# A decoder layer on Trainium2: the mixers' output loop turned, gate steps placed later, the value bank copied whole, and score tiles finished beside the value projection

## The chip, the core and the metric

The kernel runs on one core of one Trainium2 chip. A core has engines that run side by side, each with its own queue of instructions: TensorE (PE in the profile) multiplies matrices and writes to PSUM, VectorE (DVE) and ScalarE (ACT) work elementwise on PSUM and SBUF, GpSimd (POOL) works elementwise, and SyncE (SP) issues the DMAs between DRAM and SBUF. They wait for each other by semaphores. The metric is device time in microseconds (us), the median of some runs. Lower is better.

## The reference, cut to what matters

One hybrid decoder layer over 1024 tokens of width 1024, batch 1, all in float32. An mLSTM of 4 heads of 128 and a forgetting attention of 8 heads of 64 stand side by side; their outputs, joined to 1024 columns, go through `w_out`. Then follow a cross attention into 256 memory tokens (4 heads of 256) and a squared-ReLU MLP.

```python
h = rmsnorm(x, ln1[l])
z = h @ w_in[l]
ml_qk, ml_v, ml_o, ml_i, ml_f, fx_q, fx_k, fx_v, fx_f = jnp.split(z, splits, axis=-1)
...
ig = ml_i + ml_b_i[l]
lf = jax.nn.log_sigmoid(ml_f + ml_b_f[l])
mh = mlstm_chunkwise(mq, mk, mv, ig, lf)          # gates by cumulative sums of lf
mh = mh * lax.rsqrt(jnp.mean(mh * mh, axis=-1, keepdims=True) + EPS) * ml_norm
ml_out = mh * jax.nn.sigmoid(ml_o)

flf = jax.nn.log_sigmoid(fx_f + fx_b_f[l])        # forgetting attention:
s = jnp.einsum('bqhd,bkhd->bhqk', qi, k) * scale  # scores
s = s + (ci[..., :, None] - cT[..., None, :])     # plus differences of the cumulative flf
s = jnp.where(qpos[:, None] >= kpos[None, :], s, -jnp.inf)
fx_out = einsum('bhqk,bkhd->bqhd', softmax(s), v)

x = x + jnp.concatenate([ml_out, fx_out], axis=-1) @ w_out[l]
x = x + cross_attention(rmsnorm(x, ln_x[l]), rmsnorm(mem, ln_mem[l]), w_xq[l], w_xkv[l], w_xo[l])
u = jax.nn.relu(rmsnorm(x, ln2[l]) @ w_ff1[l])
x = x + (u * u) @ w_ff2[l]
```

## The kernel before, in words

**Numbers and tiles.** Activations are held transposed, features on the 128 partitions and tokens along the free axis, in 8 tiles of 128 features and two halves (`hf`) of 512 tokens. Each float32 operand is split into a high part (ACT, lines 138 and 141) and a low part, the remainder (DVE, lines 139 and 142). A product is then three matmuls, low times high, high times low and high times high (`mm3`, lines 192 to 194). PSUM has eight banks of 128x512 under five names: sc (3), tp (2), mm, m2 and ov (1 each). `mm()` hands out banks by a list of names that the stages set. SBUF buffers rotate under tags: act (7 large ones), w4 (5), z4 (2), and r_a to r_y, of which r_a and r_y have one buffer and the others two. A tile that takes a buffer waits until the former tile in it is read for the last time, a DMA out of it included.

**Who orders the work.** The program is traced in the order of the code, and the framework's scheduler then orders each engine's instructions by what is ready and by priority. Inside `in_order()` compute instructions keep the order of the code on each engine. All loads and stores are issued on one queue, SP, in its own order: a DMA that waits for a buffer holds up those behind it.

**Stages.** First the normalised input, then `token_major` for the mLSTM's values, with `row_first` and `gate_rows` called between its blocks. The gate's log-sigmoid is a polynomial on DVE (lines 449 to 453); `gate_rows` transposes the gates on TensorE (lines 469 and 474) and scans them along the tokens; `gate_cols` (lines 494 and 495) turns them back and stores the split cumulative sums in DRAM (`decay`, line 500). `mem_prepare` normalises the memory tokens, in steps that are called between others. Then the four mLSTM heads: `ml_project` makes a head's projections and `ml_head` its scores and output. Its last part, per half, loads a factor row that went through DRAM (`facd`, line 635), scales (lines 638 and 639), splits and stores the result to `mix` (lines 642 and 643).

**Forgetting attention.** `slot()` (line 1001, under `in_order`) does one step of several pipelines: a tile's scores go to a score bank by `Tile.score` (lines 748 and 749), the next slot takes their row maximum (`top`, lines 755 and 758, the second being the minimum of two negated maxima of a tile in two parts), the one after exponentiates (`exp`, lines 761 and 763), then `scale` divides (lines 768, 769 and 772). `Values` transposes the probabilities (line 787), splits them (lines 138 and 139) and multiplies them with the values (line 807), four to eight key blocks adding up in the one bank ov, rows 0 to 63 from the values' high parts and rows 64 to 127 from their low parts. `fx_close` (lines 811 to 817) joins these: ACT copies the lower 64 rows to r_c (line 816), DVE adds them to the upper 64 rows in PSUM (line 817). `fx_store` (lines 819 to 823) stores the finished pair of heads to `mix`. A first run of 13 slots does scores only, beside the end of the mLSTM; then `token_major(a["w_fv"], ...)` (line 1067) projects the values of all 8 heads in two columns of eight blocks, which `fv_sink` splits and stores to DRAM (`fvd`, line 662). The normalised memory is loaded (`hmd`, line 1069, 2 MB), and then slots with values run on, each with a piece of filler: the memory's keys and values and the part of `w_out` that needs only the first five feature tiles (`out_unit`; its sums go to `x1d`, line 945). The filler's weights are split in halves by ACT and, in turn, GpSimd and DVE (lines 974 and 975). `fv_load` (line 846) reads a head's values back.

**The mixers' output and the cross attention.** The other three feature tiles of the mixed output are loaded (`mix_load`, line 867) and multiplied in `out_proj` (line 876): per half, 8 blocks of 9 matmuls, with a weight load of 128x768 (line 180) and a split for every second block. `full_sink` (lines 1095 to 1112) loads the block's row of `x1d` into one of three tags (line 1099), adds (line 1103), stores it (line 1104), splits it for the queries (lines 141 and 142) and adds its squares (line 241). `cross_head` (line 1119) projects the queries of one head and half, 24 matmuls for each of two feature tiles, loads the head's keys and values (lines 1132 and 1133), and makes scores, softmax and output. The MLP and the last norm follow; they make up the time from about 760 us on.

## Time and profile before

| | |
|---|---|
| Runs | 1524.34, 1520.54, 1520.23 us; median 1520.54 |
| The profiled execution's own time | 1521.71 us |
| Its span, first to last instruction | 1519.7 us |
| Mean granted TensorE clock | 0.997 of full speed |
| ScalarE, VectorE, GpSimd busy | 48%, 73%, 28% |
| DMA | 298.28 MB, 196 GB/s on average |

The profile is of one execution, traced by the hardware. A timeline row gives start and duration in us, the engine, the line of the kernel, the operation, output and inputs by the program's names, shape and count, and in square brackets the engine's idle time just before with the work that ended it. A row of waits says which operation of which line waited for what: us in total, how often, and the longest. A row by stretches gives for each engine its busy time with the number of instructions, then the granted clock, the DMA share and GB/s. Shown busy times of matmuls overlap, so a busy engine isn't one at its peak.

### The profile page before, as it was taken

How to read it: one execution, taken by the hardware profiler on the slowest of the kernel's cores; microseconds unless marked ns; L12 is line 12 of the kernel's file. 1: busy time of each engine (PE TensorE's matmuls, PEld its weight loads, DVE VectorE, ACT ScalarE, POOL GpSimd, SP SyncE). 2: the span in 40 equal slices, each digit the busy share in tenths (PEclk: the TensorE clock that was granted, in tenths of full speed). 3: DMA queues.
4: the chain of work that ended last, by engine and by line, in shares of the span. 5: the costliest groups of instructions: out<-in, count | busy, mean ns of one | idle time of the engine just before them, and what ended most of it. 6: DMA issues, size and time to landing. Idle time of an engine off the chain costs nothing.

```text
span 1519.7 us, 21937 instructions
## 1 busy us (share of the span) xinstructions
PE 1502.2 (99%) x7708; PEld 1259.2 (83%) x7708; DVE 1102.4 (73%) x1745; ACT 723.1 (48%) x1349; POOL 433.1 (28%) x497
## 2 busy tenths in 40 slices
PE   9999999999999999999999999999999999999997
PEld 8888888889898888788888888788888888888887
DVE  7676676665798875854457888888887788777765
ACT  7333343334678763644343456565566432222124
POOL 0003030413455441001100033343343544343312
PEclk9999999999999999999999999999999999999998
DMA  6332333436887958953334436776775965555623
GB/s 211 118 108 91 118 101 123 133 127 174 267 248 221 302 178 283 315 197 119 118 138 156 164 122 231 280 276 241 264 262 210 366 261 222 222 222 217 253 84 111
DMA packets 118673, 298.28 MB, mean 196 GB/s; under 512 B 13202, under 2 KB 27852, under 8 KB 112420
## 3 DMA queue, kind: packets, MB, share of 16 engines
q1 hardware_dynamic: 118276, 296.79, 56.5%
q8 instruction: 60, 0.98, 0.3%
q14 instruction: 49, 0.40, 0.1%
q10 hardware_dynamic: 288, 0.11, 0.0%
HBM read 200.13 MB, written 96.72 MB: 195 GB/s over the span
## 4 chain that ended last, share of the span: by engine, by line
PE 88%; DMA 6%; DVE 3%; ACT 2%; issue 1%; SPq 0%; POOLq 0%; POOL 0%; DVEq 0%; ACTq 0%
PE tp L192 8%; PE tp L194 8%; PE tp L193 8%; PE sc L192 6%; PE sc L194 6%; PE sc L193 6%; PE m L193 6%; PE m L194 6%; PE m L192 6%; PE mm L193 5%; PE mm L192 5%; PE mm L194 5%; PE ov L192 2%; PE ov L193 2%; PE ov L194 2%; PE ov L807 2%
## 5 line engine op out<-in xcount | busy, mean ns | idle before, releaser
L192 PE MATMUL tp<-act,wl 128*128 128x512 f32 (+1 forms) x456 | 178.6, 392 | 0.0
L193 PE MATMUL tp<-act,wh 128*128 128x512 f32 (+1 forms) x456 | 178.6, 392 | 0.0
L194 PE MATMUL tp<-act,wh 128*128 128x512 f32 (+1 forms) x456 | 178.5, 392 | 0.0
L138 ACT ACTIVATE wh<-wr 128x1024 fp32r<-128x1024 f32 (+3 forms) x100 | 96.1, 962 | 118.3 <-PE tp L194 36.9
L139 DVE TENSOR_TENSOR wl<-wr,wh 128x1024 fp32r<-128x1024 f32 (+3 forms) x100 | 116.4, 1165 | 18.7 <-ACT wh L138 18.1
L192 PE MATMUL mm<-act,wl 128*128 128x512 f32 (+1 forms) x328 | 126.0, 384 | 0.7 <-DVE r_d L1103 0.7
L193 PE MATMUL mm<-act,wh 128*128 128x512 f32 (+1 forms) x328 | 125.8, 384 | 0.0
L194 PE MATMUL mm<-act,wh 128*128 128x512 f32 (+1 forms) x328 | 125.5, 383 | 0.0
L193 PE MATMUL m<-act,wh 128*128 128x512 f32 (+1 forms) x312 | 119.1, 382 | 0.7 <-DMA act<-mix 0.7
L192 PE MATMUL m<-act,wl 128*128 128x512 f32 (+1 forms) x312 | 119.3, 382 | 0.4 <-DVE r_d L1103 0.4
L194 PE MATMUL m<-act,wh 128*128 128x512 f32 (+1 forms) x312 | 119.1, 382 | 0.0
L194 PEld LDWEIGHTS tp<-act,wh 128*128 128x128 f32 x456 | 85.7, 188 | 19.5
L192 PEld LDWEIGHTS tp<-act,wl 128*128 128x128 f32 x456 | 85.7, 188 | 19.1
L193 PEld LDWEIGHTS tp<-act,wh 128*128 128x128 f32 x456 | 85.8, 188 | 19.0
L192 PE MATMUL sc<-act,wl 128*128 128x512 f32 (+1 forms) x260 | 100.7, 387 | 0.0
L193 PE MATMUL sc<-act,wh 128*128 128x512 f32 (+1 forms) x260 | 100.5, 387 | 0.0
L194 PE MATMUL sc<-act,wh 128*128 128x512 f32 (+1 forms) x260 | 100.5, 387 | 0.0
L1451 POOL TENSOR_TENSOR z<-wr 128x256 f32<-128x256 f32 x56 | 53.6, 978 | 148.4 <-DMA wr<-w_ff2q 131.7
L138 ACT ACTIVATE w<-wr 128x768 fp32r<-128x768 f32 (+2 forms) x31 | 25.5, 824 | 132.1 <-PE tp L194 69.1
L138 ACT ACTIVATE wh<-z 128x1024 fp32r<-128x1024 f32 (+2 forms) x55 | 52.5, 956 | 64.5 <-POOL z L1451 28.9
L139 DVE TENSOR_TENSOR wl<-z,wh 128x1024 fp32r<-128x1024 f32 (+2 forms) x55 | 66.1, 1202 | 10.1 <-ACT wh L138 10.1
L192 PEld LDWEIGHTS mm<-act,wl 128*128 128x128 f32 x328 | 61.6, 188 | 13.1 <-DVE r_d L1103 1.2
(677 smaller groups left out, 4187.2 us busy)
## 6 DMA issues: line engine op xcount, KB each, us to landing
act<-right SPq DMA_DIRECT2D x35, 1024.0 KB
right<-r_d SPq DMA_DIRECT2D x70, 256.0 KB
right<-w SPq DMA_DIRECT2D x56, 256.0 KB
wr<-w_ff2q SPq DMA_DIRECT2D x28, 512.0 KB
act<-fqk SPq DMA_DIRECT2D x48, 256.0 KB
wr<-w_in SPq DMA_DIRECT2D x20, 512.0 KB
wr<-w_ff SPq DMA_DIRECT2D x20, 512.0 KB
fqk<-r_p SPq DMA_DIRECT2D x32, 256.0 KB
```

The source lines that it names most:

```text
L138: s.activation(hi, src, AF.Copy)
L139: return v.tensor_tensor(out=lo, in0=src, in1=hi.bitcast(F32), op=ALU.subtract)
L192: nc.tensor.matmul(ps, w[1], x[0], start=first, stop=False, skip_group_check=more)
L193: nc.tensor.matmul(ps, w[0], x[1], start=False, stop=False, skip_group_check=more)
L194: nc.tensor.matmul(ps, w[0], x[0], start=False, stop=last, skip_group_check=more)
L807: nc.tensor.matmul(self.ov[:, c0:], self.fv[:, self.j], t[:, c0:], start=self.j == 0 and t is self.p[1], stop=self.last and t is self.p[0])
L1451: g.tensor_tensor(out=o, in0=x, in1=y, op=op)
```

## The change

Four places are changed; the matmuls that are computed stay the same.

**Gates.** `gate_rows` is called one block later (5 in place of 4), and `gate_cols` becomes the first step of the generator that prepares the memory.

**Last mLSTM head and the value projection.** In the last head both factor rows are loaded at once into two buffers (r_a, r_d), and the second half's high part goes to r_e in place of r_y. `catch_up` tops, exponentiates and scales the score tiles in flight: once ahead of the value projection and twice in each of its columns, under `in_order`. The first head's values are loaded inside the second column, and the score inputs of later heads (`fx_step`) are issued after that load.

**Slots.** `fx_close` copies the whole bank on ACT (128 rows in place of 64) and returns the addition, which `slot` issues later, after the probabilities' split; it adds two SBUF tiles. The minimum of line 758 is a `tensor_scalar` in place of a `tensor_tensor`.

**Output and first queries.** The loop over blocks is outermost and that over halves innermost, so four weight loads serve both halves. Both halves' mixed tiles are loaded first. The first query weight is loaded before the last block, the first query projection uses a score bank, the first head's scores run in another order, and the norms' rows are made later, between the cross heads.

```diff
@@ -626,18 +626,20 @@
         rsqrt_cols(fac, sqs, 1.0 / P, 8)
         v.tensor_tensor(out=fac, in0=fac, in1=rd, op=ALU.mult)
         yield
+        end = hd == MLH - 1
+        fbs = [w2("a"), w2("d")] if end else [None, None]
+        at = facd[hd : hd + 1]
         for hf in range(2):
-            fb = w2("a")
-            at = facd[hd : hd + 1]
+            fb = fbs[hf] or w2("a")
             if hf == 0:
                 to_row(fb, fac, 8, at, sc)
-            else:
-                load(fb, at[:, TH:].broadcast_to([P, TH]))
+            if hf != end:
+                load(fbs[1] or fb, at[:, TH:].broadcast_to([P, TH]))
             yield
             y = nums[hf]
             v.scalar_tensor_tensor(out=y, in0=y, scalar=vec[:, VEC["ml_norm"] + hd : VEC["ml_norm"] + hd + 1], in1=fb, op0=ALU.mult, op1=ALU.mult)
             v.scalar_tensor_tensor(out=y, in0=og[:, hf * TH : hf * TH + TH], scalar=1.0, in1=y, op0=ALU.add, op1=ALU.mult)
-            yh, yl = w2("y", dt=F32R), y.bitcast(F32R)
+            yh, yl = w2("e" if end and hf else "y", dt=F32R), y.bitcast(F32R)
             split(yh, yl, y, 0.5)
             load(mix[hf, 0, :, hd], yh.bitcast(F32))
             load(mix[hf, 1, :, hd], yl.bitcast(F32))
@@ -684,10 +686,14 @@
 
     banks[:] = ["tp", "m2", "tp", "sc", "mm", "sc", "sc"]
     turn[0] = 0
-    token_major(a["w_mv"], mv_sink, (1,), {2: row_first, 4: gate_rows}, other)
-    gate_cols()
+    token_major(a["w_mv"], mv_sink, (1,), {2: row_first, 5: gate_rows}, other)
     banks[:] = ["mm", "tp", "m2", "tp"]
-    closing = mem_prepare()
+
+    def gates_then_memory():
+        gate_cols()
+        yield from mem_prepare()
+
+    closing = gates_then_memory()
     ready = ml_project(0)
     for hd in range(MLH):
         closing = ml_head(hd, *ready)
@@ -703,7 +709,7 @@
         g.memset(t[0:2, 3].bitcast(F32), 1.0)
         stacks.append(t)
 
-    coming = []
+    coming, fetched = [], []
 
     def fx_load(hd):
 
@@ -719,7 +725,8 @@
     def fx_step():
         if coming:
             dst, src = coming.pop(0)
-            load(dst.bitcast(F32), src)
+            with tc.issue_after(fetched[0]) if fetched else nullcontext():
+                load(dst.bitcast(F32), src)
 
     masks = []
 
@@ -755,7 +762,7 @@
             v.tensor_reduce(out=self.mxs[:, e : e + 1], in_=self.ps[e], axis=mybir.AxisListType.X, op=ALU.max, negate=True)
             if e:
 
-                v.tensor_tensor(out=self.mxs[:, 1:2], in0=self.mxs[:, 0:1], in1=self.mxs[:, 1:2], op=ALU.min)
+                v.tensor_scalar(out=self.mxs[:, 1:2], in0=self.mxs[:, 1:2], scalar1=self.mxs[:, 0:1], scalar2=None, op0=ALU.min)
 
         def exp(self, e):
             s.activation(self.pt[:, slice(*self.parts[e])], self.ps[e], AF.Exp, bias=self.mxs[:, e : e + 1], accum_out=self.dens[:, e : e + 1])
@@ -813,8 +820,8 @@
             om[hf] = w2("f")
         rng = slice(hd % 2 * FXD, hd % 2 * FXD + FXD)
         t = w2("c")
-        s.activation(t[0:FXD], ov[FXD:], AF.Copy)
-        v.tensor_tensor(out=om[hf][rng], in0=ov[0:FXD], in1=t[0:FXD], op=ALU.add)
+        s.activation(t, ov, AF.Copy)
+        return lambda: v.tensor_tensor(out=om[hf][rng], in0=t[0:FXD], in1=t[FXD:], op=ALU.add)
 
     def fx_store(hd, hf):
         hi, lo = w2("y", dt=F32R), om[hf].bitcast(F32R)
@@ -843,11 +850,13 @@
 
     def fv_load(hd):
         t = w4((P, 8, P), F32R)
-        load(t.bitcast(F32), fvd[hd])
+        got = load(t.bitcast(F32), fvd[hd])
+        if not fetched:
+            fetched.append(got.ins)
         return t
 
     def value_steps():
-        fvs = {0: fv_load(0)}
+        fvs = {0: first_fv.pop()}
         for hd in range(FXH):
             for hf in range(2):
                 ov = ov_()
@@ -872,20 +881,6 @@
         for p_ in range(2):
             load(t[:, p_].bitcast(F32), mix[hf, p_, :, k])
         return t[:, 0], t[:, 1]
-
-    def out_proj(w_src, src, hf, sink):
-
...
 
     late = []
 
@@ -998,13 +993,34 @@
 
     stores, topped = [], []
 
+    def score_steps():
+        tops = scored[:]
+        scored.clear()
+        for t, e in tops:
+            t.top(e)
+        yield
+        exps = topped[:]
+        topped[:] = tops
+        for t, e in exps:
+            t.exp(e)
+        while exped:
+            exped.pop(0).scale()
+        exped.extend(t for t, e in exps if e == len(t.parts) - 1)
+
+    def catch_up():
+        with in_order():
+            mask()
+            for _ in score_steps():
+                pass
+
     def slot(values, until):
         with in_order():
             todo_ = late[:]
             late.clear()
             closing = bool(ended)
+            sums = []
             while ended:
-                fx_close(*ended[0])
+                sums.append(fx_close(*ended[0]))
                 hd, hf, _ = ended.pop(0)
                 if hd % 2:
                     stores.append((hd, hf, True))
@@ -1019,20 +1035,14 @@
                 if y.last:
                     ended.append((y.hd, y.hf, y.ov))
                     break
-            tops = scored[:]
-            scored.clear()
-            for t, e in tops:
-                t.top(e)
+            going = score_steps()
+            next(going)
             if x:
                 x.cut()
                 adds.append(x)
-            exps = topped[:]
-            topped[:] = tops
-            for t, e in exps:
-                t.exp(e)
-            while exped:
-                exped.pop(0).scale()
-            exped.extend(t for t, e in exps if e == len(t.parts) - 1)
+            for f in sums:
+                f()
+            next(going, None)
             fx_step()
             part = next(parts, None)
             if part:
@@ -1064,7 +1074,14 @@
         slot(False, 0)
         if i in (1, 11):
             next(closing, None)
-    token_major(a["w_fv"], fv_sink, between={4: lambda: next(closing, None)})
+    catch_up()
+    first_fv = []
+
+    def middle():
+        catch_up()
+        first_fv.append(fv_load(0) if first_fv else None)
+
+    token_major(a["w_fv"], fv_sink, between={1: middle, 2: catch_up, 4: lambda: next(closing, None)})
     hm = act().rearrange("p a b -> p (a b)").rearrange("p (e k c) -> p e k c", e=2, k=KT)
     load(hm.bitcast(F32), hmd)
     banks[:] = ["mm", "m2"]
@@ -1086,46 +1103,52 @@
         if step[1]:
             (step[2]() or (lambda: None))()
     banks[:] = ["mm", "tp", "m2", "tp"]
-    mix_fx = [mix_load(MLH + KX, KT, 0)]
-    h2 = []
+    mix_fx = [mix_load(MLH + KX, KT, hf) for hf in range(2)]
+    h2 = [(act(), act()) for _ in range(2)]
+    second_acc = [w2("b") for _ in range(2)]
     mix_done = []
-    for hf in range(2):
-        hi, lo = act(), act()
-        acc = w2("b")
-
...
-        out_proj(a["w_out_b"], mix_fx[hf], hf, full_sink)
-        h2.append((hi, lo))
-        acc0 = acc
-
-
-    def cross_head(hd, hf, oh, ol):
+
+    def full_sink(n, hf, ps):
+        hi, lo = h2[hf]
+        t = rotate("p", "d", "e")
+        with tc.issue_after(last_raw[0].ins):
+            load(t, x1d[hf, :, n])
+        v.tensor_tensor(out=t, in0=ps, in1=t, op=ALU.add)
+        done = load(x1d[hf, :, n], t)
+        split(hi[:, n], lo[:, n], t, vec[:, VEC["ln_x"] + n :][:, 0:1])
+        square_sum(second_acc[hf], t, n == 0)
+        if hf == 1 and n == KT - 3:
+            mix_done.append(done)
+
+    def row_second(hf):
+        at = slice(hf * TH, hf * TH + TH)
+        to_row(row[:, at], rcol[:, 4 * hf : 4 * hf + 4], 4, rowd[2:3, at])
+
+    def out_rest():
+        kn = KT - MLH - KX
+        for n in range(KT):
+            if n % CB == 0:
+                w = both(weights(a["w_out_b"][n // CB], kn * CB * P), lambda t: t.rearrange("p (k c) -> p k c", k=kn))
+            if n == KT - 1:
+                queries.append(weights(a["w_xq"][0]))
+            at_ = n % CB * P
+            for hf in range(2):
+                ps = mm()
+                for k in range(kn):
+                    mm3(ps, both(w, lambda t: t[:, k, at_ : at_ + P]), mix_fx[hf][k], k == 0, k == kn - 1)
+                full_sink(n, hf, ps)
+
+    queries = []
+    out_rest()
+
+    def cross_head(hd, hf, oh, ol, first):
         q = []
         for kk in range(2):
             t = [rotate(*tags).bitcast(F32R) for tags in ((("b",), ("c",)), (("p",), ("a", "y")))[kk]]
-            for _, _, ps in proj(weights(a["w_xq"][2 * hd + kk]), h2, 1, order=[(hf, 0)], into=ps_tile(("mm", "m2")[kk])):
+            for _, _, ps in proj(queries.pop() if queries else weights(a["w_xq"][2 * hd + kk]), h2, 1, order=[(hf, 0)], into=ps_tile(("sc" if first else "mm", "m2")[kk])):
                 split(*t, ps, 1.0 / 16.0)
+            if first and kk == 0:
+                rsqrt_sums(second_acc[0], rcol[:, 0:4], 4)
             q.append(t)
         kx, vx = w4(dt=F32R), w4(dt=F32R)
         with tc.issue_after(mix_done[0].ins):
@@ -1137,11 +1160,13 @@
         pr = z4()[:, :T].rearrange("p (i c) -> p i c", i=4)
         den, rden, mxc = col("den", 4), col("rden", 4), col("mx", 4)
         sps = [sc().rearrange("p (i c) -> p i c", i=2) for _ in range(2)]
-        for i in range(4):
+        order = [(i, kk) for i in range(4) for kk in range(2)]
+        if first:
+            order = [(i + e, kk) for i in range(2) for kk in range(2) for e in (0, 2)]
+        for i, kk in order:
             sp = sps[i // 2]
-            for kk in range(2):
-                mm3(sp[:, i % 2], both(q[kk], lambda z: z[:, i * P : (i + 1) * P]), (kx[:, 0, kk], kx[:, 1, kk]), kk == 0, kk == 1)
-            if i % 2:
+            mm3(sp[:, i % 2], both(q[kk], lambda z: z[:, i * P : (i + 1) * P]), (kx[:, 0, kk], kx[:, 1, kk]), kk == 0, kk == 1, first)
+            if i % 2 and kk:
                 v.tensor_reduce(out=mxc[:, i - 1 : i + 1], in_=sp, axis=mybir.AxisListType.X, op=ALU.max, negate=True)
 
                 v.tensor_tensor(out=mxc[:, i - 1 : i + 1], in0=mxc[:, i - 1 : i + 1], in1=rcol[:, 4 * hf + i - 1 : 4 * hf + i + 1], op=ALU.mult)
@@ -1302,17 +1327,17 @@
     for hf in range(2):
         oh, ol = act(), act()
         for hd in range(XH):
-            steps = cross_head(hd, hf, oh, ol)
+            steps = cross_head(hd, hf, oh, ol, first=not (hd or hf))
             next(steps)
             if hf and hd == XH - 1:
-                for n in range(2):
+                for n in range(3):
                     first_half(n)
             for _ in steps:
                 pass
-            if hf == 0 and hd < 2:
-                (row_second(1) if hd else rsqrt_sums(acc0, rcol[:, 4:8], 4))
+            if hf == 0 and hd < 3:
+                ((lambda: rsqrt_sums(second_acc[1], rcol[:, 4:8], 4)), (lambda: row_second(0)), (lambda: row_second(1)))[hd]()
         os_.append((oh, ol))
-    for n in range(2, KT):
+    for n in range(3, KT):
         first_half(n)
     H.update({c: h_tile() for c in ("t1", "t2")})
     for n in range(KT):
```

32 lines of the change are left out of this document (1 added, 31 removed).

## The prediction

> **What bounds the kernel now.** I read the busy times first, then busy time by stage, then what TensorE waits for, then the places themselves in the timeline.
>
> ```profile
> PE 1502.2 (99%) x7708; PEld 1259.2 (83%) x7708; DVE 1102.4 (73%) x1745; ACT 723.1 (48%) x1349; POOL 433.1 (28%) x497
> ```
> ```profile
> 44.00:60.00 16.00, 15.32 (x132) 14.73 (x131) 11.13 (x25) 6.86 (x14) 0.00 (x0) 1.00 0.19 63
> 60.00:385.00 325.00, 325.00 (x1738) 276.56 (x1737) 212.17 (x348) 123.70 (x222) 68.78 (x86) 1.00 0.40 124
> 385.00:410.00 25.00, 23.67 (x181) 21.89 (x180) 18.90 (x44) 17.55 (x47) 11.79 (x17) 1.00 0.83 262
> 410.00:575.00 165.00, 161.62 (x1089) 144.67 (x1088) 139.45 (x338) 125.46 (x344) 80.80 (x131) 1.00 0.76 236
> 575.00:605.00 30.00, 30.00 (x134) 24.30 (x133) 15.01 (x21) 9.01 (x18) 4.41 (x5) 1.00 0.91 309
> 605.00:660.00 55.00, 52.94 (x242) 42.38 (x241) 42.58 (x66) 31.17 (x51) 1.03 (x1) 1.00 0.87 304
> 660.00:1500.00 840.00, 840.00 (x3806) 685.21 (x3804) 619.74 (x810) 371.13 (x589) 257.00 (x237) 1.00 0.57 206
> 1500.00:1520.00 20.00, 11.33 (x90) 10.71 (x88) 9.59 (x28) 6.26 (x14) 5.07 (x7) 0.79 0.34 119
> ```
> ```profile
> PE sc L748 <- ACT act L761: 1.7, 3, 0.7
> ...
> PE ov L807 <- DVE r_f L817: 1.1, 2, 0.7
> PE sc L192 <- DVE r_c L142: 0.9, 1, 0.9
> PE mm L192 <- DVE r_d L1103: 0.7, 1, 0.7
> PE m L193 <- DMA act<-mix: 0.7, 1, 0.7
> PE mm L469 <- DVE w L453: 0.7, 1, 0.7
> PE tp L787 <- DVE r_e L139: 0.6, 1, 0.6
> ...
> PE m L192 <- DVE r_d L1103: 0.4, 1, 0.4
> ```
>
> TensorE bounds it: 1502.2 us of the span of 1519.7. The second fence gives stretch and length, then busy time of PE, PEld, DVE, ACT and POOL, the granted clock (1.00 but in the tail), DMA share and GB/s. All the slack lies in few places: the last 20 us (8.7 us, in code that the diff leaves alone) and four stretches that it touches: 44 to 60 (0.68 idle), 385 to 410 (1.33), the attention slots from 410 to 575 (3.38) and the mixers' output with the first cross attention, 605 to 660 (2.06). That is 7.45 us. The matmuls stay the same in number and size, so an edit is worth the waits of PE that it removes and no more; work taken from DVE, ACT or the queues counts only where PE waits for it.
>
> An idle time shown is less than what it costs:
>
> ```profile
> 636.36 0.40 PE L194 MATMUL m<-act,wh 128*128 128x512 f32 x1
> 637.49 0.50 PE L192 MATMUL mm<-act,wl 128*128 128x512 f32 x1 [0.73 <-DVE r_d L1103]
> 637.83 0.39 PE L193 MATMUL mm<-act,wh 128*128 128x512 f32 x1
> 638.07 0.39 PE L194 MATMUL mm<-act,wh 128*128 128x512 f32 x1
> ```
>
> Matmuls of this shape normally start 0.24 apart (the last two rows), though each shows 0.39 busy. Here the starts are 1.13 and 0.34 apart: lost are 0.89 and 0.10, so 0.99 for an idle time of 0.73. I add 0.27 to each stall for the pipeline that empties and fills.
>
> **The change, part by part.**
>
> *Gates.* PE waits 0.7 once for the last step of the forget polynomial (the L453 row). In the changed order ten projection matmuls of 128x256 stand ahead of those transposes (half of the 0.24 each, 1.2 us), more than the wait. With the refill: **-0.95**. The column transposes and decay stores go behind the first memory step; PE has no idle time for 325 us after, so I cost them at nothing. The cover is that stretch's slack on DVE (212 of 325) and ACT (124); without it they would cost the small transposes' waits, under 1 us.
>
> *Forgetting scores beside the value projection, and the last mLSTM head.* Stretch 385 to 410.
>
> ```profile
> 378.27 0.45 SPq L1069 DMA_DIRECT2D act<-hmd  x1
> 379.13 0.32 SPq L642 DMA_DIRECT2D mix<-r_y  x1
> ```
> ```profile
> 390.00 0.63 ACT L141 ACTIVATE r_y<-r_f 128x512 fp32r<-128x512 f32 x1 [3.38 <-DMA mix<-r_y]
> ```
> ```profile
> 406.49 0.63 ACT L974 ACTIVATE wh<-wr 128x512 fp32r<-128x512 f32 x1 [1.22 <-DMA wr<-w_xk]
> ```
>
> ACT stands still for 3.38 us until 390.00 because the head's two halves share the one y buffer, whose store sat behind the 2 MB memory load; everything behind it comes late, and PE waits three times for an exponential (L748 on L761, 1.33 idle in this stretch). After the change the second half has its own buffer, both factor loads go out early, and the three score parts are topped and exponentiated under the value blocks. Those waits go: 1.33 + 3 x 0.27 = **-2.1**; of these the third hangs on the w_xk load (406.49) and may stay (0.21 idle in its window, half a microsecond with the refill).
>
> What is late next is the first value load:
>
> ```profile
> 370.87 0.37 SPq L846 DMA_DIRECT2D w<-fvd  x1
> ```
> ```profile
> 394.16 0.48 PE L807 MATMUL ov<-r_e,w 128*128 128x512 f32 x1
> ```
> ```profile
> 378.00:396.00 18.00, 17.27 (x136) 16.16 (x135) 12.09 (x34) 10.02 (x30) 4.56 (x8) 1.00 0.99 306
> ```
>
> Before, it was issued at 370.87, ahead of the memory load, and used at 394.16. In the changed order on SP it stands behind the memory load (2.1 MB), three mix stores and three value stores (256 KB each) and is 0.5 MB itself: 4.2 MB, with what was still under way some 4.5. At 306 GB/s, with a full share of 0.99, that takes 14 to 15 us from 379: it lands between 393 and 395.5, while PE, without the stall of 0.73 + 0.27 just ahead, will ask for it near 393.2. It costs 0 to 3 us; I take **+1.0**, near the lower end because the row's own first use is at 394.16.
>
> *The value bank copied whole.*
>
> ```profile
> 425.12 0.59 ACT L816 ACTIVATE r_c<-ov 64x512 f32<-64x512 f32 x1
> 425.13 1.16 DVE L975 TENSOR_TENSOR wl<-wr,wh 128x512 fp32r<-128x512 f32 x1
> 426.31 0.69 DVE L817 TENSOR_TENSOR r_f<-ov,r_c 64x512 f32<-64x512 f32 x1
> ```
> ```profile
> 449.00:453.00 4.00, 3.90 (x28) 3.38 (x27) 3.83 (x10) 3.80 (x10) 1.97 (x2) 1.00 0.46 159
> 561.00:566.00 5.00, 4.87 (x28) 3.92 (x27) 3.37 (x8) 2.89 (x7) 2.57 (x5) 1.00 0.41 150
> ```
> ```profile
> L975 DVE TENSOR_TENSOR wl<-wr,wh 128x512 fp32r<-128x512 f32 x15 | 14.1, 943 | 1.2 <-ACT wh L974 1.1
> ```
>
> The value bank is single. PE may write it again only when DVE has added its two halves; at 425 that add stands behind a weight split of 1.16 and ends at about 427.0, though ACT had its copy at 425.7. With the bank copied whole, ACT's end releases it, 1.3 us sooner. The copy covers 128 rows of 512 in place of 64: the trace has no such copy, but 512 elements of 64 rows take 0.59 and 128-row activations from PSUM of the same length 0.60, so I cost it at nothing (both ends: 0 and 16 x 0.1). PE's waits for L817: 1.1 for two, and 0.10 and 0.13 in the windows at 450 and 563, which is four stalls of 16 closings: 1.33 + 4 x 0.27 = **-2.4**.
>
> The add now reads two SBUF tiles. Its nearest rows are the PSUM form here, 0.69, and the weight half L975, which is of that kind, mean 0.943, 1.16 above. So 16 adds cost from 0 to 16 x 0.47 = 7.5 us of DVE time, and I take the mean's 0.25 each, 4 us. DVE is busy 139.45 of 165, and PE no longer waits for this add itself; what may suffer is the next split (below). The Trainium skill ("SBUF — State Buffer", section "Who interferes with whom") says: "A DVE instruction with two SBUF inputs contends with a GpSimd instruction that reads SBUF". That speaks against this edit, and the spread from 0.69 to 1.16 fits it.
>
> ```profile
> L758 DVE TENSOR_TENSOR c_mx<-c_mx x31: 151/160/1045, 380.9 to 558.5; 128x1 f32<-128x1 f32 x31
> ```
>
> The minimum of two columns takes 0.16 at the median and once 1.045; as a tensor_scalar it may keep to its median. PE bears no wait of its own from it in the waits list, so nothing more is counted.
>
> *What stays in the slots*: 0.6 for the split L139 at 491.7, 0.7 for the mix load, and one exponential near 457 that waits for a weight load; about 2 us idle. No edit reaches them.
>
> *The output loop.* Four weight loads and splits of 128x768 in place of eight, since one serves both halves.
>
> ```profile
> 619.27 0.43 SPq L1099 DMA_DIRECT2D r_d<-x1d  x1
> ```
> ```profile
> 624.36 0.69 DVE L1103 TENSOR_TENSOR r_d<-m,r_d 128x512 f32<-128x512 f32 x1 [0.76 <-DMA r_d<-x1d]
> ...
> 635.61 1.23 DVE L139 TENSOR_TENSOR wl<-wr,wh 128x1024 fp32r<-128x1024 f32 x1 [0.77 <-ACT wh L138]
> ...
> 649.25 0.68 DVE L142 SCALAR_TENSOR_TENSOR r_c<-mm,r_b 128x512 fp32r<-128x512 f32 x1
> ```
>
> Three stalls (0.4, 0.7, 0.9). The first waits for an x1d row from DRAM; the second for a block's sum behind a query weight split; the third for the first query's low part, which stands behind the rest of the loop's sums on DVE. After: DVE loses four splits (near 1 us each), the first query weight comes earlier, the first query goes to a score bank, so it does not wait for the loop's banks, and the next projection (24 matmuls, 5.6 us) stands between it and the first scores: DVE may be over 4 us later than in this trace. The queue carries 4 x 393 KB = 1.6 MB less (5 us at 304 GB/s). All three go: 2.06 + 3 x 0.27 = **-2.9**.
>
> **Sum.** -0.95 - 2.1 - 2.4 - 2.9 = -8.35; the value load +1.0; and as PE comes earlier to places that hang on the w_xk, w_xv and mix loads, and DVE's adds grow, I expect some of it again: one stall of 1.0 (the stalls seen cost 0.4 to 1.2 each). So **-6.3**. The profiled execution took 1521.71, its span 1519.7 with 2.0 around it: 1515.4 by its own time. It lies 1.2 above the median of 1520.54; from that, 1514.2.
>
> **Rivals.**
>
> 1. *The waits move.* The slots' operands come in a fixed rhythm from ACT, DVE and the queue; PE, released early, waits at the next one. For: DVE 85% and ACT 76% busy there, DMA share 0.76. Against: of 165 us PE idles 3.38, and of 16 closings 12 show no wait at all, so operands are mostly well ahead. Half of the 8.35 goes: **1517**.
> 2. *The value load is 3 us late.* For: the full queue share of 0.99. It costs 2 more than I took, and the scores behind it are delayed once: **1516.5**.
> 3. *The new adds meet GpSimd.* POOL is busy 80.8 of 165, so about half of 16 are stretched by 0.47 or more; if five of them make the next split late as at 491.7 (0.6 + 0.27), 4.4 comes back: **1518.6**. It is the mechanism of the skill's rule above. Against: with 15 such weight splits already there, one PE wait is of this kind.
> 4. *The output loop becomes bound by its rows*, the slower side. Rows move through six buffers. A load takes 5.1 us (619.27 to 624.36); with the sum (0.7) and a store, which I estimate alike, a buffer is held 10.9 us, while six blocks of nine matmuls take 12.6. Both mix loads (1.6 MB each) now stand ahead, at a queue share of 0.91. If transfers take half again as long, a buffer is held 16.0: 3.4 lost in each round, 16/6 rounds, 9 us, and the 2.9 is not gained: 1514.2 + 2.9 + 9 = **1526**. It decides from 12.6 us, that is, transfers of 6 us each. Against: fewer bytes in all.
> 5. *The edits do nothing at their places*, PE being held by the same loads: **1520.5**.
>
> **How the numbers follow.** Forecast (1511 to 1516) 0.62; rival 1 0.12; 2 0.06; 3 0.07; 4 0.08; 5 0.05. The low end is the full 8.35 and one of the slots' other waits gone (1.0 with its refill, and a little): 1511. The high end takes in rivals 1, 2, 3 and 5, to 1521. Measurement tells about 0.3% (4.6 us) from no change, so faster is below 1516.0: the forecast's 0.62 and a share of rivals 1 and 2, 0.65; slower, above 1525.1: most of rival 4, 0.07; within: 0.28.
>
> **What would show it.** Right: no PE wait on L453; PE busy over 24.7 in the stretch that held the 385 to 410 work, with no wait on L761; no wait of the value bank on DVE; PE full from the output loop to the first scores. Wrong: a PE wait for w from fvd near 393; PE waits on L139 behind adds of over 1 us; output sums that wait for x1d on DVE and PE waiting for them; a sum of PE idle time outside the tail above 4 us.

## The result, and the profile after

The changed kernel is slower by a little: 1523.1 us (median; 1519.94 to 1527.42) beside 1520.94 of the kernel before (1519.28 to 1524.34), a ratio of 1.0016 with a 95% interval of 1.0009 to 1.0024. The forecast was 1514.2. (A ratio here is the record's, from all executions; it need not be that of the two medians.) The profiled execution took 1526.98 with a span of 1525.2; it is one of the longer ones, and the reason for that is part of the answer.

Waits of TensorE in the changed kernel (what waited for what: us in total, times, longest):

```profile
PE m L192 <- DVE r_p L1116: 2.8, 1, 2.8
PE tp L794 <- DVE r_e L139: 1.7, 3, 0.7
...
PE sc L755 <- ACT act L768: 1.6, 1, 1.6
PE ov L814 <- DMA w<-fvd: 1.6, 1, 1.6
```

Every wait that the change aimed at is gone from this list: the polynomial (L453), the value bank's addition (L817, now L824), the exponentials near 390 and the two waits on the output loop's sums and the query split. Others stand in their place. Those of 2.8 for a row's sum (L1116) and 1.6 for the first value load are new. The 1.6 for an exponential (L768, at 461) is an old wait that grew; the prediction had named it as out of reach of the edits:

```profile
457.34 0.50 PE L748 MATMUL sc<-act 128*128 128x512 f32 x1 [0.74 <-ACT act L761]
```
```profile
461.45 0.49 PE L755 MATMUL sc<-act 128*128 128x512 f32 x1 [1.65 <-ACT act L768]
```

(The first row is of the kernel before.) The waits for a split of the probabilities (L139) also grew, from one of 0.6 to three, 1.7 together.

By stretches (busy PE, PEld, DVE, ACT, POOL, then clock, DMA share, GB/s):

```profile
44.00:60.00 16.00, 16.00 (x138) 15.50 (x138) 10.36 (x25) 5.91 (x13) 0.00 (x0) 1.00 0.19 68
60.00:385.00 325.00, 324.77 (x1734) 275.97 (x1733) 214.49 (x351) 124.32 (x222) 66.73 (x85) 1.00 0.40 122
385.00:410.00 25.00, 23.00 (x167) 21.09 (x166) 15.71 (x38) 14.95 (x41) 9.37 (x15) 0.93 0.91 275
410.00:575.00 165.00, 161.18 (x1090) 144.43 (x1088) 141.88 (x339) 124.47 (x349) 85.83 (x134) 1.00 0.77 234
605.00:660.00 55.00, 52.19 (x217) 41.76 (x216) 39.31 (x61) 27.84 (x42) 1.95 (x1) 0.94 0.78 262
```

The gates' stretch is full now (16.00 for 15.32). In the stretches from 385, 410 and 605 TensorE is idle for longer than before (2.00, 3.82 and 2.81 for 1.33, 3.38 and 2.06), and in the first and the last of these the clock is below 1. From 44 to 660 the idle time is 8.9 in place of 7.45: the prediction's own sign of being wrong was more than 4. The timeline around the longest wait shows why the clock counts:

```profile
642.49 0.40 PE L194 MATMUL sc<-act,wh 128*128 128x512 f32 x1
645.69 0.79 PE L192 MATMUL m<-act,wl 128*128 128x512 f32 x1 [2.81 <-DVE r_p L1116]
646.28 0.63 PE L193 MATMUL m<-act,wh 128*128 128x512 f32 x1
646.71 0.63 PE L194 MATMUL m<-act,wh 128*128 128x512 f32 x1
```
```profile
645.00:652.00 7.00, 6.31 (x15) 4.96 (x16) 5.56 (x8) 1.35 (x2) 0.00 (x0) 0.51 0.92 345
```

After the wait matmuls start 0.43 apart (646.28 to 646.71) in place of 0.23; the granted clock is 0.51 from 645 to 652. The wait lost 3.0 us, and the half clock behind it about another 2.8 (one matmul by 0.36, thirteen by 0.19).

What made the sum L1116 late is found on the DMA queue:

```profile
633.58 0.32 SPq L1115 DMA_DIRECT2D r_e<-x1d  x1
633.95 0.42 SPq L1117 DMA_DIRECT2D x1d<-r_p  x1
...
634.90 0.44 SPq L1155 DMA_DIRECT2D w<-kxd  x1
635.39 1.10 SPq L1156 DMA_DIRECT2D w<-vxd  x1
636.60 0.40 SPq L180 DMA_DIRECT2D wr<-w_xq  x1
638.63 0.32 SPq L1115 DMA_DIRECT2D r_p<-x1d  x1
```
```profile
631.49 0.69 DVE L1116 TENSOR_TENSOR r_p<-mm,r_p 128x512 f32<-128x512 f32 x1
...
644.94 0.69 DVE L1116 TENSOR_TENSOR r_p<-m,r_p 128x512 f32<-128x512 f32 x1 [3.99 <-issue]
```

The last row's load can be issued only when its buffer's store (633.95) has landed, at 638.63, and then has 1.5 MB of keys, values and query weights ahead of it. It lands at about 644.9, 6.3 us later. (The profile names no releaser for the sum, only "issue"; that it waited for this load is inferred, as the load is what it still lacked, and the experiments below bear it out.) The turned loop places the sixth block of the second half, whose store lets the keys go, four blocks from the end in place of two.

The queue's other late transfer, the first value load, is the one that the prediction named:

```profile
373.49 0.38 SPq L664 DMA_DIRECT2D fvd<-r_b  x1
379.03 0.37 SPq L664 DMA_DIRECT2D fvd<-r_p  x1
...
388.15 1.12 SPq L853 DMA_DIRECT2D w<-fvd  x1
```
```profile
375.00:380.00 5.00, 5.00 (x43) 4.87 (x42) 3.83 (x9) 1.45 (x3) 0.04 (x1) 1.00 0.36 111
```

It is issued at 388.15, behind nearly 4 MB since 380 (the memory load, four mix stores and three value stores), and is there at about 396.1, when the first matmul that reads it starts. Ahead of that burst nothing is issued for 5.5 us: the queue stands behind one value store whose data VectorE has not made yet, at a DMA share of 0.36.

```profile
SPq L664 <- DVE r_p L142: 5.1, 1, 5.1
```

In the kernel before the value load had been issued at 370.87, and the same stretch has:

```profile
375.00:380.00 5.00, 5.00 (x42) 4.82 (x41) 2.68 (x5) 2.28 (x7) 0.69 (x1) 1.00 0.61 181
```

### The profile page after: what moved, and what is told of

Its sections match the earlier page's. It is cut to its first block, busy times and chain, and to the rows that moved or that the text cites. A ratio compares the mean times of both kernels' runs of the same rounds, so it can differ in the third digit from the quotient of the medians.

```text
span 1525.2 us, 21910 instructions
## 1 busy us (share of the span) xinstructions
PE 1505.5 (99%) x7708; PEld 1262.2 (83%) x7708; DVE 1097.5 (72%) x1741; ACT 717.0 (47%) x1345; POOL 440.7 (29%) x497
## 4 chain that ended last, share of the span: by engine, by line
PE 64%; DVE 2%; issue 1%; DMA 1%; ACT 0%; POOL 0%; SPq 0%; POOLq 0%; DVEq 0%; ACTq 0%
PE sc L193 6%; PE sc L192 6%; PE sc L194 6%; PE tp L194 5%; PE tp L192 5%; PE tp L193 5%; PE m L193 4%; PE m L192 4%; PE m L194 4%; PE mm L192 4%; PE mm L193 4%; PE mm L194 4%; PE ov L192 2%; PE ov L194 2%; PE ov L193 2%; PE ov L814 1%
## 5 line engine op out<-in xcount | busy, mean ns | idle before, releaser
L138 ACT ACTIVATE wh<-wr 128x1024 fp32r<-128x1024 f32 (+3 forms) x96 | 92.6, 966 | 102.2 <-PE tp L194 34.1
L139 DVE TENSOR_TENSOR wl<-wr,wh 128x1024 fp32r<-128x1024 f32 (+3 forms) x96 | 111.6, 1164 | 20.3 <-ACT wh L138 20.2
L192 PE MATMUL mm<-act,wl 128*128 128x512 f32 (+1 forms) x320 | 122.8, 384 | 0.0
L193 PE MATMUL mm<-act,wh 128*128 128x512 f32 (+1 forms) x320 | 122.4, 383 | 0.0
L194 PE MATMUL mm<-act,wh 128*128 128x512 f32 (+1 forms) x320 | 122.3, 382 | 0.0
L192 PE MATMUL sc<-act,wl 128*128 128x512 f32 (+1 forms) x268 | 103.8, 387 | 0.0
L193 PE MATMUL sc<-act,wh 128*128 128x512 f32 (+1 forms) x268 | 103.7, 387 | 0.0
L194 PE MATMUL sc<-act,wh 128*128 128x512 f32 (+1 forms) x268 | 103.6, 387 | 0.0
L139 DVE TENSOR_TENSOR wl<-z,wh 128x1024 fp32r<-128x1024 f32 (+2 forms) x55 | 64.6, 1176 | 10.2 <-ACT wh L138 10.2
L192 PEld LDWEIGHTS m<-act,wl 128*128 128x128 f32 x312 | 59.3, 190 | 15.1 <-DVE r_p L1116 3.2
```

Of the source, the lines that this page charges most:

```text
L138: s.activation(hi, src, AF.Copy)
L139: return v.tensor_tensor(out=lo, in0=src, in1=hi.bitcast(F32), op=ALU.subtract)
L192: nc.tensor.matmul(ps, w[1], x[0], start=first, stop=False, skip_group_check=more)
L193: nc.tensor.matmul(ps, w[0], x[1], start=False, stop=False, skip_group_check=more)
L194: nc.tensor.matmul(ps, w[0], x[0], start=False, stop=last, skip_group_check=more)
```

## Experiments

Each time is a median; "before" is the kernel before on the same chip beside it. These medians of before differ by up to 1.3 us from session to session, so kernels that were not measured beside each other are compared by their ratios (the changed kernel: 1.0016). The clock is the granted clock, averaged over the executions; it was 0.9975 or 0.9976 for the kernel before in each of these sessions and 0.9963 for the changed kernel.

| Kernel | us | before | ratio, 95% interval | clock |
|---|---|---|---|---|
| rows_first | 1521.96 | 1521.88 | 1.0005 [0.9996, 1.0015] | 0.9969 |
| value_early | 1526.02 | 1521.88 | 1.0036 [1.0023, 1.0049] | 0.9956 |
| both | 1524.44 | 1521.88 | 1.0028 [1.0017, 1.0040] | 0.9960 |
| both_tile | 1523.31 | 1521.88 | 1.0009 [1.0000, 1.0017] | 0.9962 |
| value_hole | 1522.28 | 1521.30 | 1.0003 [0.9994, 1.0012] | 0.9969 |
| rows_eight | 1520.44 | 1521.30 | 0.9992 [0.9984, 1.0001] | 0.9973 |
| all_three | 1518.03 | 1521.30 | 0.9976 [0.9965, 0.9986] | 0.9973 |
| close_only | 1522.36 | 1521.30 | 1.0000 [0.9991, 1.0010] | 0.9975 |
| no_close | 1516.36 | 1520.54 | 0.9969 [0.9958, 0.9981] | 0.9977 |
| no_catch | 1517.41 | 1520.54 | 0.9981 [0.9972, 0.9990] | 0.9975 |
| no_gates | 1517.89 | 1520.54 | 0.9979 [0.9970, 0.9988] | 0.9974 |
| loop_only | 1519.33 | 1520.75 | 0.9991 [0.9982, 1.0000] | 0.9978 |
| loop_as_changed | 1520.05 | 1520.75 | 0.9995 [0.9982, 1.0007] | 0.9974 |
| no_close_catch | 1517.48 | 1520.75 | 0.9981 [0.9973, 0.9990] | 0.9973 |

Theory A: the gain was there and was eaten by transfers that the change makes late on the one DMA queue, and by half clock behind the long waits. Theory B: PE waits only move; curing one brings the next.

**The keys behind the last row** (rows_first; the edits shown here are cut, and the remarks behind # are added).

```diff
-        if hf == 1 and n == KT - 3:
-            mix_done.append(done)      # done: the block's store
+        if hf == 1 and n == KT - 1:
+            mix_done.append(got)       # got: the block's row load
```

> The changed kernel, with one edge on the DMA queue moved: the first head's keys and values (1 MB) are issued behind the last x1d row's load in place of behind the store of the sixth block of the second half. Everything computed and the order on the engines stay the same. Theory A (the changed kernel's gain is eaten by two late transfers, and each long wait of TensorE is followed by matmuls at half clock): the wait of 2.8 us for the sum L1116 at 645.7 and the fifteen matmuls 0.43 apart behind it go, 3.0 + 2.9 us; 1517 to 1519.5. Theory B (waits only move: the rows' six buffers bind the loop, the last row is late with or without the keys): 1521 to 1523.

The wait went from 2.8 to 1.1 and no half clock followed:

```profile
PE m L192 <- DVE r_p L1116: 1.1, 1, 1.1
```

By the ratios (1.0016 to 1.0005, with intervals that overlap) about 1.7 us came back, less than the 3.6 to 6.1 of theory A, and the median lies in theory B's range. So the keys were part of the lateness, not all of it. Nor does every execution of the changed kernel pay all of the half clock that its profile shows. The record has the granted clock of each of its 22 executions: the four at 0.995, to which the profiled one belongs, took 1526.9 on average, the ten at 0.996 took 1523.8, the six at 0.997 took 1523.0 and the two at 0.998 took 1521.0. Of the 106 executions of the kernel before beside these experiments 103 have 0.997 or 0.998.

**The first value load early**, in two forms. In value_early the last head's mix stores, the later value stores and the memory load were tied behind it; in value_hole only the load was moved into the gap, and the rest kept its order.

```diff
 value_early
+        with tc.issue_after(fetched[0]) if fetched else nullcontext():   # in fv_sink, the value stores
+        behind(fetched[0], held[-4:])          # the last head's mix stores
+    with tc.issue_after(fetched[0]):
+        got = load(hm.bitcast(F32), hmd)       # the 2 MB memory load
+    behind(got.ins, held_fv[-4:])              # the last four value stores
 value_hole
+    queue = [held_fv[9], held_fv[10], held[-4], load(hm.bitcast(F32), hmd), held[-2], held[-3], held[-1], *held_fv[11:14]]
+    for x, y in zip([fetched[0], *(i.ins for i in queue)], queue):
+        behind(x, [y])
```

(`behind(first, rest)` orders the DMAs of `rest` behind `first` on the queue. In value_hole two more such edges put the last two value stores behind the third and the sixth score load, as they stand in the changed kernel.)

> The changed kernel, with the DMA queue's order changed between 370 and 395: the first value load stands ahead of the last head's four mix stores, the later value stores and the 2 MB memory load. The order on TensorE stays the same. Theory A: the wait of 1.6 us for w from fvd at 396.0 and the slow matmuls after it go, 1.7 + 0.6 + about 1.5 us; 1519 to 1521. Theory B: the exponentials or the memory load are late in its place; 1522 to 1523.

> The changed kernel; on the DMA queue only the first value load is moved, into the gap of 5.5 us (373.5 to 379.0) in which the queue waits for a value store's data; the memory load and the rest keep their places (the second head's value load comes two places earlier). The order on the engines is the same. Theory A (a stage bound by bytes on the queue between 380 and 400, which lost its head start in that gap): 0.5 MB are moved in an empty time, so the wait at 396 goes and no other takes its place: about 1.7 + 0.6 below the changed kernel, more where the clock had dropped: 1519 to 1521. Theory B (any reordering of this queue makes another transfer late, as the earlier trial did with the key weights): 1523 to 1526.

value_early is the slowest of all. The wait at 396 is gone, and a longer one came, on ACT's weight half:

```profile
410.14 0.63 ACT L976 ACTIVATE wh<-wr 128x512 fp32r<-128x512 f32 x1 [5.05 <-DMA wr<-w_xk]
```
```profile
411.77 0.79 PE L762 MATMUL sc<-act 128*128 128x512 f32 x1 [4.05 <-ACT act L775]
```

The chain of that profile shows the transfer behind it:

```profile
402.05 8.07 DMA wr<-w_xk
```

With the memory load held until 385.1, this weight load was issued at 402.05 and took 8.1 us. In value_hole the first value load went out in the gap with nothing else held back; the weight load was issued at the same time (401.98), but was there at 405.6, and the stretch came out nearly full:

```profile
405.56 0.63 ACT L979 ACTIVATE wh<-wr 128x512 fp32r<-128x512 f32 x1 [0.56 <-DMA wr<-w_xk]
```
```profile
385.00:410.00 25.00, 24.57 (x186) 22.54 (x185) 18.80 (x43) 18.14 (x50) 11.93 (x17) 1.00 0.86 262
```

So what counts between 380 and 410 is how much still stands in the queue: here the early load helped where it used time in which the queue had been empty, and harmed where it displaced another. value_early missed both theories' ranges on the slow side, value_hole (1522.28) lies between them. By the ratios value_hole is about 2.0 us below the changed kernel, though its profile still has the late row (2.5 idle) with 3.4 us of half clock behind it.

**Both edits, and the fifth tile's loads behind the weights** (both, both_tile).

```diff
 both_tile
     def mix_tile(k, hf):
+        with tc.issue_after(last_raw[0].ins):
             for p_ in range(2):
                 load(t[:, p_].bitcast(F32), mix[hf, p_, :, k])
```

> Both edits of the queue together. Theory A: the two add up, and the four cured places of the diff show: 1513 to 1517, no stretch of matmuls at half clock outside the start and the tail. Theory B: 1519 to 1522.

> Both edits of the queue, and the loads of the mixed tile of the fifth feature block (z from mix, 256 KB each) behind the newest raw weight load, so that they don't hold up the weights in the queue while they wait for a mix store. Theory A: the wait for an exponential near 460 (1.65 idle, behind a weight load that landed late) goes too, about 1 to 1.8 us below the kernel with both edits: 1512 to 1515.5. Theory B (the weight load is late because its buffer is free late): the same as the kernel with both edits, within 0.5.

Both carry value_early's wait for the key weights (2.9 and 4.3 of TensorE), so their medians are above the kernel before and miss both theories. The tile edit did its part: in the changed kernel ACT waits 3.62 at 459.83 for a weight that stood in the queue behind a tile load which waited for a mix store; with the edit the same wait is 0.28. (In the kernel before it is 2.87; this is the wait at 457 and 461 above.)

```profile
459.83 0.63 ACT L969 ACTIVATE wh<-wr 128x512 fp32r<-128x512 f32 x1 [3.62 <-DMA wr<-w_xv]
```
```profile
457.82 0.63 ACT L977 ACTIVATE wh<-wr 128x512 fp32r<-128x512 f32 x1 [0.28 <-DMA wr<-w_xv]
```

**Eight row buffers** (rows_eight, with the keys behind the last row).

```diff
-        t = rotate("p", "d", "e")
+        t = rotate("p", "d", "e", "f")
```

> The changed kernel with the keys behind the last row's load, and eight buffers in place of six for the x1d rows (the tag f is free there). Theory A (the rows' buffers bind the end of the loop: load, sum, store and again load): the wait of 1.1 us for the sum L1116 before the second query projection goes too; 0.8 to 1.5 below the kernel with the keys moved alone: 1520 to 1521.2. Theory B (the last row is late because of the bytes ahead of it): no more than 0.3 below it.

```profile
605.00:660.00 55.00, 55.00 (x254) 45.12 (x253) 42.45 (x66) 29.03 (x44) 1.95 (x1) 1.00 0.76 266
```

The loop and the first queries now run without a wait, and theory A's number came out: 1520.4. With the keys last, the six buffers were what still held the loop's end.

**All cures together** (all_three: eight buffers, keys last, value load in the gap, tile behind the weights).

> The changed kernel with eight row buffers, the keys behind the last row, the first value load in the gap, and the loads of the fifth feature tile behind the weights. Theory A: the cures add up, 2.3 + 2.5 + 1 below the changed kernel's 1523.1: 1516 to 1518.5, clearly below the kernel before. Theory B: PE waits for the next transfer each time: 1520 to 1522.

1518.0, below before by 0.24% with an interval clear of 1, and in the range of theory A.

```profile
385.00:410.00 25.00, 24.14 (x182) 21.91 (x181) 18.78 (x42) 17.64 (x49) 11.93 (x17) 1.00 0.89 262
410.00:575.00 165.00, 163.18 (x1097) 146.03 (x1096) 142.30 (x341) 123.82 (x345) 83.43 (x131) 1.00 0.79 240
```

**The parts alone, and undone.** close_only is the kernel before with the bank's copy and the later addition; no_close, no_catch and no_gates are the cured kernel with one part undone (each part's own lines of the diff taken back), no_close_catch with two.

> The kernel before with one part of the change alone: ACT copies the whole value bank, and DVE's addition comes after the probabilities' split. Theory A (the prediction's step): the four waits for L817 go, 2.4 us; 1518.5 to 1520 beside 1521.9 of before. Theory B (what the bank no longer waits for is waited for at the next weight or exponential): 1521 to 1522.5, with the waits for L817 gone and the waits for exponentials and splits longer by about as much.

```profile
PE sc L748 <- ACT act L761: 2.3, 3, 1.0
...
PE m L192 <- DVE r_d L1106: 1.4, 1, 1.4
...
PE tp L787 <- DVE r_e L139: 0.9, 1, 0.9
```

In close_only no wait for the bank's addition is left, and the waits for exponentials (1.7 before) and for the split (0.6) grew; the time is that of before, as theory B had it. (The interval, 0.9991 to 1.0010, leaves room for 1.4 us, not for 2.4.)

> The kernel with all the cures (1518.0), with the value bank's closing as before: ACT copies 64 rows, DVE adds from PSUM ahead of the transposes. Theory A (the prediction's step: the closings cost four waits, 2.4 us): 1519.8 to 1521. Theory B (what close_only showed: PE waits about as long for the next late operand): 1517.5 to 1519.

> The kernel with all the cures, without the catch-up of the score tiles beside the value projection; the last head's two buffers and the queue's order stay. Theory A (the prediction's step: three waits for exponentials between 390 and 410 hang on it): 1519.5 to 1520.5, those waits back. Theory B (the waits came from the shared buffer and the store, which stay cured): 1517.5 to 1518.7.

> The kernel with all the cures, with the gate steps where they were before. Theory A (the prediction's step, 0.95 for the wait on the polynomial's last step): 1518.7 to 1519.3, with the wait of 0.7 back. Theory B (another wait of that stage takes its place): within 0.3 of 1518.0.

> The kernel with all the cures without the bank's copy and without the catch-up. Theory A (both cost about as much as they bring): 1515.5 to 1516.8, like the kernel without the bank's copy, the fastest so far. Theory B (the catch-up is needed where the bank is closed as before): 1517.5 to 1519.

Undoing the bank's copy did not cost the 2.4 us that the prediction gave it: no_close has the lowest ratio of all, 0.9969, with the bank's wait back in its list (1.1). For this part theory B holds; whether the copy even costs a microsecond the intervals don't tell (0.9969 and 0.9976 overlap).

Undoing the gates or the catch-up changes the ratio by 0.0003 and 0.0005. The intervals reach 0.0009 to either side, so these times can't tell the 0.95 us of the gates (0.0006) from nothing. The traces show more. no_gates has the wait on the polynomial back (0.7). no_catch has the three waits for exponentials back (0.73, 0.38 and 0.31, before 0.73, 0.39 and 0.21), though the last head keeps its two buffers:

```profile
PE sc L765 <- ACT act L778: 1.0, 2, 0.7
...
PE sc L765 <- ACT w L778: 0.4, 1, 0.4
```

TensorE idles 1.41 and 2.25 between 385 and 410 without the catch-up (no_catch, no_close_catch), 0.86 and 0.43 with it (all_three, no_close), and no_close_catch has a ratio of 0.9981 where no_close has 0.9969, about 1.8 us, with intervals that overlap. So the second buffer alone doesn't remove the first two of these waits and the catch-up does, as the prediction had it (the third, near 407, stays in all_three too, as it had allowed); what that is worth in time is not settled.

**The turned loop alone on the kernel before**, with the cures (loop_only) and as the change has it (loop_as_changed).

> The kernel before with the turned output loop alone, with eight row buffers and the keys behind the last row. Theory A (the loop, once its rows are in time, carries nearly all of the cured kernel's gain): the loop's stretch without a PE wait, 2.9 less; 1517.2 to 1518.3. Theory B (the gain in the cured kernels came as much from the stretch 385 to 410 and the slots): 1518.6 to 1520.5.

> The kernel before with the turned output loop alone as the change has it: six row buffers, the keys behind the sixth block's store. Theory A (the late row is of the loop's own making): the wait of 2 to 3 us before the second query projection, in some executions with half clock behind it; the same as before or up to 2 slower, 1520.5 to 1522.5. Theory B (the row is late only because other parts of the change shift the loop against the queue): 1517.5 to 1519.

As changed, the loop alone has the late sum too:

```profile
PE m L192 <- DVE r_p L1100: 1.6, 1, 1.6
```

So the late row is of the loop's own making; in time it is the same as before (0.9995). With the cures the stretch from 605 to 660 is full (55.00 for 52.94), which is the 2.06 and three stalls of the prediction. The ratio is 0.9991, about 1.4 us, in theory B's range, with an interval from 0 to 2.7 us. In that profile the stretch 44 to 60 is 1.41 idle for 0.68 before, at a place that this edit doesn't touch, so idle times of single profiles vary by about this much.

**What a wait costs** (wait_ladder: idle additions ahead of the bank's release, in six closings of the kernel before).

```diff
+        for _ in range(hd + 1 if hf == 0 and 0 < hd < 7 else 0):
+            v.scalar_tensor_tensor(out=t[0:FXD], in0=ov[0:FXD], scalar=0.0, in1=t[0:FXD], op0=ALU.mult, op1=ALU.add)
```

> The kernel before with 3 to 7 (and 2) idle DVE operations of 64x512, estimated at 0.68 us each from the addition L817, ahead of that addition in the first half's closing of heads 1 to 6: six waits of TensorE in one profile, growing from about 1 to 5 us. It measures what a wait costs beyond its idle time. Theory A (the changed kernel's profile: 2.8 idle, then 6 us of matmuls 0.43 apart): waits over about 2.5 us are followed by some us at half clock, each costing 2 to 3 us more; the sum over the kernel before is 18.4 of added operations less the slack, plus 2 to 3 for each of the three or four longest. Theory B (the wait's length doesn't decide; what counts is how it falls in a running window of a few us): long waits without a drop and short ones with it; no drop at all is possible, then the sum is 13 to 18.

Two of the six waits:

```profile
429.17 0.47 PE L807 MATMUL ov<-r_e,w 128*128 128x512 f32 x1 [1.84 <-DVE r_f L819]
```
```profile
513.12 0.47 PE L807 MATMUL ov<-r_e,w 128*128 128x512 f32 x1 [2.71 <-DVE r_f L819]
```

In every profile of this case the drops of the clock to 0.5 begin whole multiples of 3.41 us apart, and ahead of the kernel's tail a half clock lasts one such step or two. Here is the ladder's profile cut into these steps, around the waits of 1.84, 2.39, 2.71 and 4.11:

```profile
426.17:429.58 3.41, 1.57 (x13) 1.31 (x12) 3.31 (x5) 2.33 (x7) 1.25 (x2) 1.00 0.43 138
429.58:432.99 3.41, 3.41 (x13) 2.92 (x12) 3.34 (x10) 2.31 (x5) 1.04 (x2) 0.50 0.37 133
480.78:484.19 3.41, 1.58 (x15) 1.33 (x13) 3.00 (x5) 2.00 (x6) 1.17 (x1) 1.00 0.22 77
484.19:487.61 3.42, 2.86 (x18) 2.58 (x19) 3.35 (x8) 2.12 (x5) 0.00 (x0) 1.00 0.11 8
508.09:511.50 3.41, 2.32 (x21) 2.07 (x19) 2.89 (x6) 2.54 (x7) 1.41 (x2) 1.00 1.05 393
511.50:514.91 3.41, 1.79 (x9) 1.57 (x10) 3.33 (x7) 1.04 (x2) 0.14 (x1) 1.00 0.91 377
535.39:538.81 3.42, 1.44 (x11) 1.01 (x9) 3.09 (x6) 1.98 (x6) 1.34 (x2) 1.00 0.73 240
538.81:542.22 3.41, 1.28 (x3) 1.12 (x4) 3.31 (x6) 0.05 (x1) 0.00 (x0) 0.50 0.99 389
```

The waits of 1.84 and 2.36 us lay inside one step, which left TensorE busy for 1.57 and 1.06 us of its 3.41, and in the next step the clock was 0.5. Those of 2.39 and 2.71 were cut in two by the end of a step (busy 1.58 and 2.86; 2.32 and 1.79), and the clock stayed. The step with 1.57 was followed by a drop and the one with 1.58 was not, so near that edge the busy time shown here doesn't decide alone. The waits over 4 us (4.11 and 4.47) dropped the clock for two steps. The two shorter drops cost half a step each, 1.7 us, the longer ones, in part idle themselves, some 2.3 and 2.7.

The one execution took 1546.2, 25.7 over before, for 18.5 us of waits in the list. So theory A's price is right and its sum fits (theory B had 13 to 18), and theory B is right that below some 3 us a wait's length doesn't decide: it is how the wait falls in the steps.

## Why the prediction was wrong, point by point

**Right.** TensorE bounds the kernel, and the four places were the ones with waits; each wait that an edit was to remove went. A refill of about 0.27 a stall holds: at 461.45 the starts are 2.04 and 0.34 apart, 1.9 lost for an idle time of 1.65. DVE's new addition takes 0.907 on average, as read from L975's 0.943, and 16 cost 3.6 us more of DVE time (14.5 for 10.9), where 4 was taken:

```profile
L824 DVE TENSOR_TENSOR r_f<-r_c 64x512 f32<-64x512 f32 x16 | 14.5, 907 | 1.3 <-ACT r_c L823 0.8
```

That the stretched additions make a split late for TensorE (rival 3) is not seen: no addition stood ahead of the three splits that it waited for; those at 414.59 and 495.89 stood behind other splits, of 1.25 and 1.66. The minimum as a tensor_scalar takes 0.214 at the median and 0.217 at most, where the tensor_tensor took 0.160 and once 1.045; nothing was counted for it.

**The step that failed first: "All three go: -2.9"** in the output loop. The three went and a fourth of 2.8 came. The prediction had written down its mechanism (rival 4: rows through six buffers, bound from 12.6 us a round) and gave it 0.08, because it found "fewer bytes in all". What counts isn't the bytes of the stage but what stands ahead of one row. The tag has two buffers, and one turn of this buffer, from its sum at 631.49 to its next at 644.94, took 13.45 us, over the 12.6 in which the prediction wanted it back: 0.7 for the sum, 1.8 until the store was issued, 4.7 until the next load could be, and 6.3 for that load. Neither transfer is half again as long as the 5.1 of the prediction; a store that stood behind a blocked load, and 1.5 MB that the turned loop lets go earlier, were enough. Of a moved step its DMAs were counted, but not that the edge "keys behind the sixth block" moves with the loop's order. The size was right in the traces: with the keys last and eight buffers the stretch has no idle time in any of the profiles (rows_eight, all_three, loop_only and the four with parts undone).

**The value load, "+1.0"**, was the right thing and the wrong size. The load was there at 396.1, past the 393 to 395.5 of the estimate, and the wait is 1.6, within its 0 to 3; but one step of half clock behind it cost another 1.7. The stretch lost about 2.1 us against before in place of gaining 1.1 (0.67 more idle, 1.7 for the clock, one refill less). That the queue stands empty just ahead of the burst, the place for the cure, was not seen.

**The closings, "-2.4"**, were waits that hid later ones. Alone they bring nothing that could be measured (1.0000). In the changed kernel their 1.33 of idle time is gone from the slots, and yet the slots idle for 3.82 in place of 3.38: the exponential behind the weight load took 0.9 more, and splits that TensorE had not waited for took the rest. The prediction kept one stall of 1.0 for all such effects together; here the whole step was such an effect (its rival 1, with 0.12).

**The gates, "-0.95"**: the wait went and came back when the step was undone; its worth in the cured kernel is less than can be measured.

**The missing term** is the clock. In the kernel before no single wait that the change touches is over 0.92 us and the clock is 1.00 in all those stretches, so a stall looked like its idle time and a refill. At 1.6 or 2.8 us it cost about double. Which executions pay that is chance: the same wait for the first value load was 1.57 in the changed kernel's profile and 1.61 in that of rows_eight, with a drop, and 1.77 in that of rows_first without one. On average the changed kernel's clock is 0.9963 where that of before is 0.9976; over 1523 us that is about 2.0 us (an estimate from figures rounded to 0.001, those of before from the later sessions), nearly all of the 2.2 by which it is slower. The forecast gain of 6.3 was lost to waits: those that grew or were new came to as much as those removed.

With the queue put right the change is worth 0.24% (0.31% without the bank's copy), by the medians 3.3 to 4.2 us, about half of the 8.35. (The queue edits are part of this; the tile's place also cures a wait that the kernel before has.) The loop alone measured 1.4 of it, with an interval that reaches nothing. How the rest divides between the catch-up, the last head's two buffers, the minimum and the tile's place stays open, and with it why the parts' waits come to more than the time.

## What to carry to other kernels

When a loop is turned or a step moved, follow the edges of the DMA queue that name a place in the old order ("behind the sixth block's store"): they move with it. For each transfer that something waits for, count the bytes and the blocked issues ahead of it in the queue, and look for empty stretches of the queue just before a burst; the early load paid there and nowhere else in these runs. A wait that is removed is worth its length only if the operand behind it is shown to be early, so try the part alone. And read the granted clock of every execution: here it told which of them paid for a long wait.

## What the runs showed of the hardware

The drop to half clock came after waits of TensorE as short as 1.6 us (changed kernel, at 396: clock 0.5 from 395.86 to 399.27) and 1.84 us (ladder), and did not after 1.77 (rows_first), 2.39 and 2.71 (ladder) and 2.88 (both); after 4.05 to 4.47 it came each time. The drops of one profile begin whole multiples of 3.41 us apart (ladder: 429.58, 456.89, 538.81 and 569.53, with 8, 24 and 9 steps between them) and last one step or two: 3.4 us at 429, 6.8 at 645. From 10 us to the tail of all these profiles, TensorE was busy for no more than 1.68 us of the step before a drop began, and a step with 1.74 or more had none behind it; between 1.57 and 1.68 both are seen.

The Trainium skill ("TensorE: Matmul & The Clock Gate", section "What's actually happening") has a window of 3.4 us that is "free-running". The 3.41 us of these steps and the mixed outcomes between 1.6 and 2.9 agree with that. The Trainium skill's advice on the same page of no gaps over about 3 us (section "Why this matters for your kernels") is too generous for these waits: here two of the four between 1.8 and 2.8 in the ladder lost the clock, and so did one of 1.57 in the changed kernel.
